# Where the tiles of an fp32r layer start in SBUF, and the form of its up-projection products

## The chip, the cores and the metric

The kernel runs on one core of one Trainium2 chip. The metric is the device time of one execution in microseconds (us). A profile belongs to one execution: its span goes from the first to the last instruction of the program, and the time of that execution contains a little more.

## The reference: what is computed

One decoder layer on x of 256 tokens by 2048 channels, all float32:

```
h   = rmsnorm(x, attn_norm_g)
z   = h @ w_in                   # pool channels | q | k | v | indexer q, k, weights
A   = pool_mixer(pool channels)  # causal means over 2, 4, 8, 16 tokens, then 256x256 products
B   = dsa_attention(q, k, v, ...)  # indexer scores, top 64 keys per query, softmax, 8 heads of 128
x1  = x + concat(A, B) @ w_out
up  = rmsnorm(x1, ffn_norm_g) @ w_up             # 2048 x 11264
c   = conv_b + causal depthwise conv of up, width 3
out = x1 + (silu(c[:, :5632]) * c[:, 5632:]) @ w_down   # 5632 x 2048
```

The weights are 203 MB, each is read once.

## The kernel before, in words

**Products in three parts.** To come near float32 accuracy, each operand is split into a high part (rounded to the fp32r type) and a low part (the rest), and a product is the sum of three: high by high, high by low and low by high, accumulated in PSUM. The split activations are the tiles `xhl` (16 row blocks of 128 channels, two parts, 256 tokens; 2048 bytes per block and partition), `yhl` (the mixer's and attention's output, same shape) and `ghl` (44 row blocks for w_down). `xhl` holds x first; after the out-projection the parts of x1 are written to the same tile (`x1_tr`, L608, by `split_x`, L119). The weights come in units of up to 1 MB through the sync engine's DMA queue into two `raw` buffers; a `Piece` (L93) is half a unit: ScalarE (ACT) rounds it into `whi` (L105), VectorE (DVE) subtracts into `wlo` (L106), with four buffers each, two pieces ahead of TensorE.

**Two roles.** In the token-major products (`mm_tok`, L210, products L222 to L224) the activations are the stationary operand, 128 tokens at a time, and a weight row of up to 512 columns moves: q, k, v and the indexer's columns (on `xhl`), the out-projection (on `yhl`) and the down-projection (on `ghl`). In the feature-major ones the weights are stationary, 128 columns at a time, and the 256 tokens move: the pool channels (`mm_feat1`, L231, three products of 256 columns, L233 to L235) and w_up (`mm_feat`, L226: one product of 512 columns with the two activation parts side by side, L228, and one of 256, L229). The products of the pool mixer (`pool_mix`, L579) use `mm_feat1` too. Each product brings its own load of the 128x128 stationary operand. The plain fp32 products and transposes of attention (L471, L483, L511, L523) run as two passes each.

**Order.** A loop at the end of `hybrid_kernel` walks over 385 pieces: per step it loads the unit three pieces ahead, splits the piece two ahead, runs the side work hung on this step by `at(step, ...)`, and then issues the piece's products. The order is w_in (indexer, k, pool, q, v interleaved), w_out, w_up for 44 blocks of 128 gate and 128 value columns, w_down in four groups of 512 columns. Attention, top-k and pooling are side work. In w_up the only side work on TensorE is `rows` of the second norm (L171, four passes of 128 columns, at its fifth step). A "block" below is one 128-row block of the contraction in w_up or in the pool channels: one stationary high part, one low part.

**After w_up's products.** Because high by high and high by low lie in separate halves of a 512-column PSUM row, `up_out` (L631) adds the halves: an ACT copy (L635), a DVE add (L636) and a DVE multiply by the norm's factor (L637) into `up`. `up_conv` and `up_gate` then make `ghl`.

**Places.** A tile's start in SBUF follows from what was allocated before it. Modulo 512 bytes, `xhl` starts at 256, `yhl` at 192, `ghl`, `whi` and `wlo` at 64 in this kernel. The blocks are multiples of 512 bytes, so all blocks of such a tile, both parts and both halves of the tokens start at the same place; a moving weight row of 512 columns does too.

Of the kernel before, what the change touches and what calls it, by code (L numbers as in the profile page):

```python
# [8 lines left out]
F32 = mybir.dt.float32  # L9
F32R = mybir.dt.float32r  # L10
BF16 = mybir.dt.bfloat16
AF = mybir.ActivationFunctionType
ALU = mybir.AluOpType
AX = mybir.AxisListType

P = 128
S = 256
D = 2048
KT = D // P
IH = 16  # L20
DFF = 5632
NF = DFF // P
# [7 lines left out]
C_AG, C_FG, C_PS, C_QG, C_KG, C_IC, C_CW, C_CB = 0, 16, 32, 40, 41, 42, 58, 58 + 3 * 2 * NF  # L30
# [9 lines left out]
WARM = 8  # L40


@with_exitstack
def hybrid_kernel(ctx, tc, xT, xN, par, wIa, wIb, wIc, wI2, wA, wU, wP, wO, wUp, wDn, out):
    nc = tc.nc
    PS = bass.MemoryType.PSUM

    cp = ctx.enter_context(tc.tile_pool(name="cp", bufs=1))
# [4 lines left out]
    pr = cp.tile([P, C_N], F32, name="pr")  # L53

    xf = cp.tile([P, KT, S], F32, name="xf")
    xt = xf.rearrange("p k t -> p (k t)").rearrange("p (a d) -> p a d", a=2)
    xhl = cp.tile([P, KT, 2, S], F32R, name="xhl")
    ga = cp.tile([P, KT], F32, name="ga")


# [32 lines left out]
    class Piece:  # L93


        def __init__(self, unit, a, b, mm):
            self.unit, self.a, self.b, self.mm = unit, a, b, mm
# [18 lines left out]
        sides.setdefault(step, []).append(lambda: f(*a))  # L116


    def split_x(k, src, gains, on_act):  # L119
        g = gains[:, k:k + 1]  # L120
        if on_act:
            nc.scalar.activation(xhl[:, k, 0], src, AF.Copy, scale=g)  # L122
        else:
            nc.vector.tensor_scalar(xhl[:, k, 0], src, g, None, op0=ALU.mult)
        nc.vector.scalar_tensor_tensor(xhl[:, k, 1], src, g, xhl[:, k, 0].bitcast(F32),  # L125
                                       op0=ALU.mult, op1=ALU.subtract)

    zp = ctx.enter_context(ExitStack())
    zc = zp.enter_context(tc.tile_pool(name="zc", bufs=1))
# [48 lines left out]
    r1, r2 = TokenNorm("r1"), TokenNorm("r2")  # L178
# [46 lines left out]

    def mm_feat(o, wh, wl, rhs, first, last):  # L226

        nc.tensor.matmul(o, wh, rhs.rearrange("p a t -> p (a t)"), start=first, stop=False)  # L228
        nc.tensor.matmul(o[:, 0:S], wl, rhs[:, 0], start=False, stop=last)  # L229

    def mm_feat1(o, wh, wl, rhs, first, last):  # L231

        nc.tensor.matmul(o[:, 0:S], wh, rhs[:, 0], start=first, stop=False)  # L233
        nc.tensor.matmul(o[:, 0:S], wh, rhs[:, 1], start=False, stop=False)  # L234
        nc.tensor.matmul(o[:, 0:S], wl, rhs[:, 0], start=False, stop=last)  # L235

    def tok_chunk(srcs, width, cuts=()):

        acc = Acc()
        for q in range(4):  # L240
            u = Unit(srcs[q], 4 * width, cuts[q] if q < len(cuts) else None)
            for h in range(2):
                def mm(p, k0=4 * q + 2 * h):
                    mm_tok(acc, p, (k0, k0 + 1), width)
                pieces.append(Piece(u, 2 * h * width, (2 * h + 2) * width, mm))
        return acc


    def pool_chunk(n):
        acc = Acc()  # L250
        for j in range(2):
            u = Unit(wU[2 * n + j], D)
            for h in range(2):
                def mm(p, j=j, h=h):
                    pt = acc.get()
                    for i in range(8):
                        k = 8 * h + i
                        mm_feat1(pt[:, j], *p.get(i * P, P), xhl[:, k], k == 0, k == KT - 1)
                pieces.append(Piece(u, h * 1024, (h + 1) * 1024, mm))
        return acc  # L260

    ia, za, ua, first = [], {}, [], {}
# [17 lines left out]
    for name in ORDER:  # L280
# [9 lines left out]
        else:  # L290
            c = ("k0", "k1", "q0", "q1", "v0", "v1").index(name)
            za[name] = tok_chunk([wA[c, q] for q in range(4)], 512)


    yhl = zc.tile([P, KT, 2, S], F32R, name="yhl")
    oa = []
    O0 = len(pieces)
    for c in range(4):
        acc = Acc()
        oa.append(acc)  # L300
        for q in range(4):
            u = Unit(wO[c, q], 2048)
            for h in range(2):
                def mm(p, acc=acc, k=4 * q + 2 * h):
                    mm_tok(acc, p, (k, k + 1), 512, yhl)
# [4 lines left out]
    for f in range(NF):  # L310
        us = [Unit(wUp[2 * f + j], D) for j in range(2)]
        seq = [(j, h) for j in range(2) for h in range(2)]
        if f == 0:
            seq = [(0, 0), (1, 0), (0, 1), (1, 1)]
        for j, h in seq:
            def mm(p, f=f, j=j, h=h):
                pt = ga_[f].get()
                for i in range(8):
                    k = 8 * h + i
                    mm_feat(pt[:, j], *p.get(i * P, P), xhl[:, k], k == 0, k == KT - 1)  # L320
            pieces.append(Piece(us[j], h * 1024, (h + 1) * 1024, mm))

    da = [Acc() for c in range(4)]
# [1 line left out]
    ghl = None  # L325
    for c in range(4):
        for m in range(NF // 2):
# [5 lines left out]
            o = (m % 2) * 1024  # L333
# [195 lines left out]
    pw_ = {}  # L529
# [49 lines left out]
    def pool_mix(n):  # L579
        g = GROUPS[n]  # L580
        hi, lo = pwt[n]
        for j in range(2):
            pt = ps_s.tile([P, 512], F32, name="pm", tag="ss")
            for k in range(2):
                c = slice(k * S + j * P, k * S + j * P + P)
                mm_feat1(pt, hi[:, c], lo[:, c], pw_[n][:, k], k == 0, k == 1)
            sc = pr[:, C_PS + 2 * g + j:C_PS + 2 * g + j + 1]
            y = yhl[:, 4 + 2 * n + 4 * (n == 3) + j]
            nc.scalar.activation(y[:, 0], pt[:, 0:S], AF.Copy, scale=sc)
            nc.vector.scalar_tensor_tensor(y[:, 1], pt[:, 0:S], sc, y[:, 0].bitcast(F32),  # L590
                                           op0=ALU.mult, op1=ALU.subtract)
# [16 lines left out]
    def x1_tr(c):  # L608
        for k in range(4 * c, 4 * c + 4, 2):
            tp = ps_s.tile([P, 512], F32, name="tp", tag="ss")  # L610
            for i in range(2):
                for th in range(2):
                    nc.tensor.transpose(tp[:, (2 * i + th) * P:(2 * i + th + 1) * P],  # L613
                                        xt[:, th, (k + i) * P:(k + i + 1) * P], ident)
            for i in range(2):
                split_x(k + i, tp[:, i * S:(i + 1) * S], pr[:, C_FG:C_FG + KT], True)


    fw = {}

    def ffn_open():
        nonlocal ghl
        zp.close()
        fp = ctx.enter_context(tc.tile_pool(name="fp", bufs=1))
        ghl = fp.tile([P, NF, 2, S], F32R, name="ghl")
        fw["up"] = [fp.tile([P, 2, S + 2], F32, name=f"up{i}") for i in range(2)]
        for u in fw["up"]:
            nc.gpsimd.memset(u[:, :, 0:2], 0.0)
        fw["fp"] = fp

    def up_out(f):  # L631
        fp = fw["fp"]
        pt = ga_[f].get()
        t = fp.tile([P, 2, S], F32, name="ft", tag="ft", bufs=2)
        nc.scalar.activation(t, pt[:, :, S:2 * S], AF.Copy)  # L635
        nc.vector.tensor_tensor(t, pt[:, :, 0:S], t, op=ALU.add)  # L636
        nc.vector.tensor_tensor(fw["up"][f % 2][:, :, 2:], t, r2.b2(), op=ALU.mult)  # L637

    def up_conv(f):
        u = fw["up"][f % 2]  # L640
# [62 lines left out]
    for n in range(4):  # L703
        st = first[f"u{n}"] + 4
        at(st, pool_u, n)
        at(st - 6, pool_w, n)
        at(st - 2, pool_ws, n)
        at(st + (n < 3), pool_win, n)
        at(st + 2 + 4 * (n < 3), pool_mix, n)
    for c in range(4):  # L710
        at(18 + 4 * c, load_xt, c)
        at(O0 + 8 * c + 8, x1_out, c)
        at(O0 + 8 * c + 9, x1_tr, c)
    at(G0 + 1, r2.cols_sq, ssq1)
    at(G0 + 2, r2.diag)
    at(G0 + 4, r2.rows)
    at(G0 + 2, ffn_open)
    for f in range(NF):
        st = G0 + 4 * f + 4
        at(st, up_out, f)  # L720
        at(st + 1, up_conv, f)
        at(st + 2, up_gate, f)
# [16 lines left out]
    def prep(n):  # L739
        if n < 15 and n % 2 == 1:  # L740
            for k in (n + 1, n + 2):
                split_x(k, xf[:, k], ga, True)
        if n < len(pieces):
            pieces[n].split(2 if n == 0 else 1)
        if n == 0:
            for k in range(2):
                split_x(k, xf[:, k], ga, False)
# [75 lines left out]
```

## Time and profile before

| | us |
|---|---|
| time, median of 3 runs | 1104.12 (1103.59 to 1105.32) |
| the profiled execution | 1104.05 |
| its span | 1102.2 |
| TensorE busy | 1094.5 (99%) |
| VectorE busy | 721.9 (65%) |
| ScalarE busy | 567.0 (51%) |
| mean granted TensorE clock | 0.999 |
| read from HBM | 203.25 MB, 186 GB/s |

A busy time counts the union of instructions that overlap. Matmuls are pipelined: the next begins before the shown end of the last, so their rate is read from the differences of their start times. The stages follow each other on TensorE: w_in to 265 us, w_out to 359 us, w_up to 858 us, w_down to 1098 us.

### The profile page before, as it was taken

To read this page: it belongs to the slowest core of one execution; us is meant where nothing else is said; L and a number is where in the kernel's file an instruction comes from. 1 tells how busy PE (TensorE), PEld (TensorE's weight loads), DVE (VectorE), ACT (ScalarE), POOL (GpSimd) and SP (SyncE) were. 2 spreads that over 40 slices of the span, in tenths; PEclk is the share of its full clock that TensorE was granted. 3 is DMA by queue.
4 is the path that set the end of the run, shared out by engine and by line. 5 is a ranking of instruction groups with operands and counts; after the bars stand their busy time and mean duration, and the time that the engine had idled before them with its cause. 6 is when DMAs were issued, how large, how long until landed. Compare 5 with 4: busy or idle time off the path is not lost.

```text
span 1102.2 us, 14803 instructions
## 1 busy us (share of the span) xinstructions
PE 1094.5 (99%) x5824; PEld 940.8 (85%) x5824; DVE 721.9 (65%) x1022; ACT 567.0 (51%) x797; POOL 12.9 (1%) x25
## 2 busy tenths in 40 slices
PE   8999999999999999999999999999999999999998
PEld 7988889889888888888888888888888888888886
DVE  7667867665555677777777777777777645444443
ACT  7555456654444655555555555555555433333331
POOL 0001000000000000000000000000000000000000
PEclk9999999999999999999999999999999999999999
DMA  8654564444554555555555555555555556565652
GB/s 284 245 190 141 180 235 153 163 163 157 186 174 171 191 192 190 181 180 181 189 187 191 191 189 182 181 180 190 187 191 191 191 191 210 191 210 191 215 191 91
DMA packets 32693, 206.30 MB, mean 187 GB/s; under 512 B 3696, under 2 KB 4080, under 8 KB 9584
## 3 DMA queue, kind: packets, MB, share of 16 engines
q1 hardware_dynamic: 31328, 203.25, 54.3%
q10 hardware_dynamic: 1296, 2.11, 0.5%
q8 instruction: 46, 0.75, 0.3%
q14 instruction: 23, 0.19, 0.1%
HBM read 203.25 MB, written 2.10 MB: 186 GB/s over the span
## 4 chain that ended last, share of the span: by engine, by line
PE 98%; DMA 1%; DVE 0%; ACT 0%; SPq 0%; issue 0%; DVEq 0%; ACTq 0%
PE mm L228 30%; PE mm L229 15%; PE mm L224 15%; PE mm L223 15%; PE mm L222 15%; PE mm L233 1%; PE mm L234 1%; PE mm L235 1%; PE sp L397 1%; DMA raw<-in_wI_dram 1%; DMA raw<-in_wIa_dram 1%; PE sp L483 0%; PE tp L613 0%; PE tp L471 0%; PE op L523 0%; PE tp L387 0%
## 5 line engine op out<-in xcount | busy, mean ns | idle before, releaser
L106 DVE TENSOR_TENSOR wlo<-raw,whi 128x1024 fp32r<-128x1024 f32 (+4 forms) x385 | 462.7, 1203 | 316.5 <-ACT whi L105 314.4
L105 ACT ACTIVATE whi<-raw 128x1024 fp32r<-128x1024 f32 (+4 forms) x385 | 400.1, 1041 | 440.9 <-PE mm L224 218.1
L228 PE MATMUL mm<-xhl,whi 128*128 128x512 f32 x1408 | 497.8, 397 | 0.0
L229 PE MATMUL mm<-xhl,wlo 128*128 128x256 f32 x1408 | 395.7, 281 | 0.0
L228 PEld LDWEIGHTS mm<-xhl,whi 128*128 128x128 f32 x1408 | 264.7, 188 | 65.3
L229 PEld LDWEIGHTS mm<-xhl,wlo 128*128 128x128 f32 x1408 | 264.3, 188 | 0.1
L222 PE MATMUL mm<-whi,ghl 128*128 128x512 f32 x352 | 136.9, 389 | 0.0
L224 PE MATMUL mm<-whi,ghl 128*128 128x512 f32 x352 | 136.9, 389 | 0.0
L223 PE MATMUL mm<-wlo,ghl 128*128 128x512 f32 x352 | 136.9, 389 | 0.0
L222 PE MATMUL mm<-whi,xhl 128*128 128x512 f32 (+3 forms) x288 | 108.6, 377 | 1.4 <-ACT xhl L122 0.8
L224 PE MATMUL mm<-whi,xhl 128*128 128x512 f32 (+3 forms) x288 | 107.3, 373 | 0.0
L223 PE MATMUL mm<-wlo,xhl 128*128 128x512 f32 (+3 forms) x288 | 106.8, 371 | 0.3 <-DVE wlo L106 0.3
L224 PEld LDWEIGHTS mm<-whi,ghl 128*128 128x128 f32 x352 | 66.1, 188 | 13.9
L222 PEld LDWEIGHTS mm<-whi,ghl 128*128 128x128 f32 x352 | 66.1, 188 | 13.8
L223 PEld LDWEIGHTS mm<-wlo,ghl 128*128 128x128 f32 x352 | 66.1, 188 | 13.5
L222 PEld LDWEIGHTS mm<-whi,xhl 128*128 128x128 f32 x288 | 54.1, 188 | 9.5 <-issue 1.2
L224 PEld LDWEIGHTS mm<-whi,xhl 128*128 128x128 f32 x288 | 54.1, 188 | 8.4 <-DVE xhl L125 0.5
L223 PEld LDWEIGHTS mm<-wlo,xhl 128*128 128x128 f32 x288 | 54.1, 188 | 8.0 <-DVE wlo L106 0.9
L222 PE MATMUL mm<-whi,yhl 128*128 128x512 f32 x128 | 50.9, 398 | 0.0
L224 PE MATMUL mm<-whi,yhl 128*128 128x512 f32 x128 | 50.5, 395 | 0.0
L223 PE MATMUL mm<-wlo,yhl 128*128 128x512 f32 x128 | 50.5, 394 | 0.0
L654 ACT ACTIVATE ghl<-fc 128x256 fp32r<-128x256 f32 x44 | 18.4, 418 | 57.0 <-DVE fc L653 57.0
(148 smaller groups left out, 843.9 us busy)
## 6 DMA issues: line engine op xcount, KB each, us to landing
raw<-in_wUp_dram SPq DMA_DIRECT2D x88, 1024.0 KB, 4.9
raw<-in_wDn_dram SPq DMA_DIRECT2D x44, 1024.0 KB, 4.9
raw<-in_wA_dram SPq DMA_DIRECT2D x24, 1024.0 KB, 4.9
raw<-in_wO_dram SPq DMA_DIRECT2D x16, 1024.0 KB, 4.9
raw<-in_wU_dram SPq DMA_DIRECT2D x8, 1024.0 KB, 4.9
raw<-in_wI_dram SPq DMA_DIRECT2D x4, 640.0 KB, 4.6
raw<-in_wIb_dram SPq DMA_DIRECT2D x3, 784.0 KB, 4.9
xf<-in_xT_dram SPq DMA_DIRECT2D x8, 256.0 KB, 5.2
```

What stands on the lines that cost most here:

```text
L105: i1 = nc.scalar.activation(hi, raw, AF.Copy)
L106: i2 = nc.vector.tensor_tensor(self.lo[:, c:c + n], raw, hi.bitcast(F32), op=ALU.subtract)
L222: nc.tensor.matmul(o, a[:, k, 0, t], wh, start=(k == 0), stop=False)
L223: nc.tensor.matmul(o, a[:, k, 0, t], wl, start=False, stop=False)
L224: nc.tensor.matmul(o, a[:, k, 1, t], wh, start=False, stop=(k == n - 1))
L228: nc.tensor.matmul(o, wh, rhs.rearrange("p a t -> p (a t)"), start=first, stop=False)
L229: nc.tensor.matmul(o[:, 0:S], wl, rhs[:, 0], start=False, stop=last)
L233: nc.tensor.matmul(o[:, 0:S], wh, rhs[:, 0], start=first, stop=False)
L234: nc.tensor.matmul(o[:, 0:S], wh, rhs[:, 1], start=False, stop=False)
L235: nc.tensor.matmul(o[:, 0:S], wl, rhs[:, 0], start=False, stop=last)
L397: nc.tensor.matmul(sp[:, a:b], q, kiT[:, e, 0:b - a], start=(e == 0), stop=(e == 1))
L654: nc.scalar.activation(ghl[:, f, 0], c[:, 0], AF.Copy)
```

## The change

A function `placed` allocates a tile with some more columns and gives a view that starts `o` float32 columns into it. With the offsets of `PLACE` x moves by 128 bytes to 384 modulo 512, `yhl` by 192 bytes to 384, and `ghl` by 320 bytes to 384. x1's parts get a view of their own in the same allocation as x, at offset 0, so they stay at 256. The weights' halves stay at 64. `mm_feat` is removed and `mm_feat1` takes its name, so a w_up block is three products of 256 columns, all added in the same 256 columns of PSUM. `up_out` has nothing left to add: one DVE multiply reads PSUM directly.

```diff
+PLACE = {"x": 32, "x2": 0, "y": 48, "g": 80}
+
+def placed(pool, n, name, o, of=None):
+    m = n * 2 * S
+    t = of[0] if of else pool.tile([P, m + (128 if name == "xhl" else o)], F32R, name=name)
+    return t, t[:, o:o + m].rearrange("p (k a t) -> p k a t", k=n, a=2)
...
-    xhl = cp.tile([P, KT, 2, S], F32R, name="xhl")
+    xhl = placed(cp, KT, "xhl", PLACE["x"])
+    x2hl = placed(cp, KT, "xhl", PLACE["x2"], xhl)
+    xhl, x2hl = xhl[1], x2hl[1]
...
-        nc.tensor.matmul(o, wh, rhs.rearrange("p a t -> p (a t)"), start=first, stop=False)
-        nc.tensor.matmul(o[:, 0:S], wl, rhs[:, 0], start=False, stop=last)
-
-    def mm_feat1(o, wh, wl, rhs, first, last):
-
         nc.tensor.matmul(o[:, 0:S], wh, rhs[:, 0], start=first, stop=False)
         nc.tensor.matmul(o[:, 0:S], wh, rhs[:, 1], start=False, stop=False)
         nc.tensor.matmul(o[:, 0:S], wl, rhs[:, 0], start=False, stop=last)
...
-    yhl = zc.tile([P, KT, 2, S], F32R, name="yhl")
+    yhl = placed(zc, KT, "yhl", PLACE["y"])[1]
...
-                    mm_feat(pt[:, j], *p.get(i * P, P), xhl[:, k], k == 0, k == KT - 1)
+                    mm_feat(pt[:, j], *p.get(i * P, P), x2hl[:, k], k == 0, k == KT - 1)
...
-                split_x(k + i, tp[:, i * S:(i + 1) * S], pr[:, C_FG:C_FG + KT], True)
+                split_x(k + i, tp[:, i * S:(i + 1) * S], pr[:, C_FG:C_FG + KT], True, x2hl)
...
-        ghl = fp.tile([P, NF, 2, S], F32R, name="ghl")
+        ghl = placed(fp, NF, "ghl", PLACE["g"])[1]
...
     def up_out(f):
-        fp = fw["fp"]
         pt = ga_[f].get()
-        t = fp.tile([P, 2, S], F32, name="ft", tag="ft", bufs=2)
-        nc.scalar.activation(t, pt[:, :, S:2 * S], AF.Copy)
-        nc.vector.tensor_tensor(t, pt[:, :, 0:S], t, op=ALU.add)
-        nc.vector.tensor_tensor(fw["up"][f % 2][:, :, 2:], t, r2.b2(), op=ALU.mult)
+        nc.vector.tensor_tensor(fw["up"][f % 2][:, :, 2:], pt[:, :, 0:S], r2.b2(), op=ALU.mult)
```

## Rows read from the trace of the kernel before

**Rows 1.** The page's busy times (part 1) and its chain of waits by line (part 4).
```profile
PE 1094.5 (99%) x5824; PEld 940.8 (85%) x5824; DVE 721.9 (65%) x1022; ACT 567.0 (51%) x797; POOL 12.9 (1%) x25
...
PE 98%; DMA 1%; DVE 0%; ACT 0%; SPq 0%; issue 0%; DVEq 0%; ACTq 0%
PE mm L228 30%; PE mm L229 15%; PE mm L224 15%; PE mm L223 15%; PE mm L222 15%; PE mm L233 1%; PE mm L234 1%; PE mm L235 1%; PE sp L397 1%; DMA raw<-in_wI_dram 1%; DMA raw<-in_wIa_dram 1%; PE sp L483 0%; PE tp L613 0%; PE tp L471 0%; PE op L523 0%; PE tp L387 0%
```

**Rows 2.** Stretch of w_up: us; busy PE, PEld, DVE, ACT, POOL; PEclk; DMA share; GB/s.
```profile
359.50:858.50 499.00, 499.00 (x2830) 433.59 (x2829) 375.76 (x530) 280.94 (x402) 0.84 (x3) 1.00 0.55 187
```

**Rows 3.** Instructions by line: ns (min/median/max), first and last start, forms.
```profile
L228 PE MATMUL mm<-xhl,whi x1408: 388/397/483, 359.5 to 858.0; 128*128 128x512 f32 x176
...
L222 PE MATMUL mm<-whi,ghl x352: 389/389/398, 858.3 to 1097.0; 128*128 128x512 f32 x176
```

**Rows 4.** Timeline of TensorE in w_up: start us, us, instruction.
```profile
599.68 0.40 PE L228 MATMUL mm<-xhl,whi 128*128 128x512 f32 x1
...
605.68 0.40 PE L228 MATMUL mm<-xhl,whi 128*128 128x512 f32 x1
```

**Rows 5.** Timeline of TensorE, pool products in a quick stretch.
```profile
115.93 0.28 PE L233 MATMUL mm<-xhl,whi 128*128 128x256 f32 x1
...
118.99 0.28 PE L233 MATMUL mm<-xhl,whi 128*128 128x256 f32 x1
```

**Rows 6.** Timeline of TensorE, pool products in a lagging stretch, and before it.
```profile
171.37 0.82 PE L483 MATMUL sp<-qk 128*128 128x128 f32 x4
...
172.38 0.28 PE L233 MATMUL mm<-xhl,whi 128*128 128x256 f32 x1
...
177.33 0.28 PE L233 MATMUL mm<-xhl,whi 128*128 128x256 f32 x1
```

**Rows 7.** Timeline of TensorE, pool products behind token-major products.
```profile
252.45 0.40 PE L224 MATMUL mm<-whi,xhl 128*128 128x512 f32 x1
252.69 0.28 PE L233 MATMUL mm<-xhl,whi 128*128 128x256 f32 x1
...
253.39 0.28 PE L233 MATMUL mm<-xhl,whi 128*128 128x256 f32 x1
...
253.73 0.28 PE L233 MATMUL mm<-xhl,whi 128*128 128x256 f32 x1
```

**Rows 8.** Timeline of TensorE, token-major products on xhl.
```profile
107.69 0.39 PE L222 MATMUL mm<-whi,xhl 128*128 128x512 f32 x1
...
110.44 0.39 PE L222 MATMUL mm<-whi,xhl 128*128 128x512 f32 x1
```

**Rows 9.** Timeline of TensorE, token-major products on yhl.
```profile
325.87 0.40 PE L222 MATMUL mm<-whi,yhl 128*128 128x512 f32 x1
...
329.35 0.40 PE L222 MATMUL mm<-whi,yhl 128*128 128x512 f32 x1
```

**Rows 10.** Timeline of TensorE, token-major products on ghl.
```profile
999.79 0.39 PE L222 MATMUL mm<-whi,ghl 128*128 128x512 f32 x1
...
1002.51 0.39 PE L222 MATMUL mm<-whi,ghl 128*128 128x512 f32 x1
```

**Rows 11.** Timeline of TensorE, plain fp32 products, two passes each.
```profile
264.92 0.59 PE L523 MATMUL op<-pT,zv 128*128 128x256 f32 x2
265.35 0.38 PE L524 MATMUL op<-pT,zv 128*128 128x128 f32 x2
```

**Rows 12.** Timeline of TensorE, the pool mixer's products.
```profile
140.92 0.28 PE L233 MATMUL pm<-dhl,pwh 128*128 128x256 f32 x1
...
142.00 0.39 PE L222 MATMUL mm<-whi,xhl 128*128 128x512 f32 x1
```

**Rows 13.** Longest wait in 380:850 (total, times, longest); the evacuation's two instructions.
```profile
ACT whi L105 <- PE mm L228: 149.8, 123, 1.6
...
L635 ACT ACTIVATE ft<-mm x44: 579/579/592, 373.1 to 859.4; 128x512 f32<-128x512 f32 x44
...
L636 DVE TENSOR_TENSOR ft<-mm,ft x44: 683/684/685, 374.1 to 860.7; 128x512 f32<-128x512 f32 x44
```

More of the change, by code (lines that the diff above doesn't have):

```diff
@@ L116, in at, with split_x @@
         sides.setdefault(step, []).append(lambda: f(*a))
-    def split_x(k, src, gains, on_act):
+    def split_x(k, src, gains, on_act, xhl=xhl):
         g = gains[:, k:k + 1]
@@ L257, in mm @@
                         k = 8 * h + i
-                        mm_feat1(pt[:, j], *p.get(i * P, P), xhl[:, k], k == 0, k == KT - 1)
+                        mm_feat(pt[:, j], *p.get(i * P, P), xhl[:, k], k == 0, k == KT - 1)
                 pieces.append(Piece(u, h * 1024, (h + 1) * 1024, mm))
@@ L585, in pool_mix @@
                 c = slice(k * S + j * P, k * S + j * P + P)
-                mm_feat1(pt, hi[:, c], lo[:, c], pw_[n][:, k], k == 0, k == 1)
+                mm_feat(pt, hi[:, c], lo[:, c], pw_[n][:, k], k == 0, k == 1)
             sc = pr[:, C_PS + 2 * g + j:C_PS + 2 * g + j + 1]
```

## The prediction

> **What bounds the kernel now.** I read the page's busy shares and its chain of waits first [rows 1]: TensorE is busy for 1094.5 of 1102.2 us, and 98% of the chain that ended last is TensorE work, with the w_up products (L228 and L229) at 45% and the three token-major products (L222 to L224) at another 45%. Nothing else is late over any length, so the time is the number of products times the spacing of their starts. The row by stage comes next [rows 2]: through w_up the granted clock is 1.00 of full speed, the 2.4 GHz level, and the DMA engines are busy 55% of the time. Nothing is lost to the clock. Then the first and last start of a kind of product [rows 3] and the timeline of TensorE, where the reader has to subtract start times (a matmul's shown length, 0.28 or 0.40 us, overlaps its successor and is no spacing):
>
> - w_up: 599.68 to 605.68 us holds 17 blocks of one 512- and one 256-column product, 353 ns each [rows 4]. From the first to the last start, 498.5 us over 1407 blocks is 354.3 ns, so this spacing holds for the whole stage.
> - the pool products, which already have the form of three 256-column products: 115.93 to 118.99 us is nine blocks, 340 ns each [rows 5].
> - the same line, same tiles, a little later: 172.38 to 177.33 us is 14 blocks, 353.6 ns each [rows 6].
> - token-major 512-column products: on xhl 107.69 to 110.44 us is twelve, 229 ns each [rows 8]; on yhl 3.48 us for fifteen, 232 ns [rows 9]; on ghl 2.72 us for twelve, 226.7 ns [rows 10], which the first and last start confirm: 238.7 us over 351 triples [rows 3].
>
> At 2.4 GHz, 512 columns are 213.3 ns and 768 columns 320 ns. So every kind of product pays 6 to 10% over its columns, and how much differs with the tile. Per 256 columns: 113.3 (pool, quick stretches; ghl), 114.6 (xhl), 116.0 (yhl), 117.8 ns (w_up; pool, lagging stretches). Two facts of the kernel stand beside that: a weight load is issued with every product, so TensorE reads two places at once, one moving and one stationary; and the start of these reads modulo 512 bytes is fixed for each tile. By the change's words and offsets the places before are 256 for x and x1, 192 for yhl, 64 for ghl, 64 for the weights' halves. The distance (moving minus stationary, modulo 512) is 0 for ghl, 384 for yhl, 320 for xhl as stationary, and 192 for w_up and the pool products, where the weights are stationary.
>
> **The change part by part.**
>
> *Form of the w_up block.* x1 stays at 256 and the weights at 64, so a w_up block becomes exactly a pool block of before, which ran at 340 ns in twelve of its sixteen stretches of eight blocks and at 353.6 in the other four. The two rates are steady once entered. Lagging stretches began twice, both times behind the four small products of L483 [rows 6]; the pool stretches that began behind a 512-column token-major product came out quick, one after two slower blocks: 0.70 us for two, then 340 ns [rows 7]. w_up is entered from a 512-column product as well, and is broken once, after twelve blocks or so, by the four small products of L171; in 1408 blocks it has nobody else between. I take the quick rate. 1408 x (353.3 - 340) = 18.7 us off. The bounds: 0 at the lagging rate; +7 us if a block took three times the 120 ns of the pool mixer's products, 1.08 us for nine, the slowest 256-column ones there are [rows 12]; -18.7 us is the most that a product of this kind shows; at 3 x 107.5 = 322.5 ns a block, what 256 cycles of the fp32 passes take [rows 11] (0.43 us for two passes of 512 cycles each), it would be -43 us.
>
> [...]
>
> *Evacuation of w_up.* The two halves no longer need adding: 44 ACT copies of 579 ns and 44 DVE adds of 684 ns go [rows 13], and the DVE multiply reads PSUM itself, which I price like the removed add (one PSUM and one SBUF operand, 684 ns). That is 25.5 us of ACT and 30.1 us of DVE saved off the path: ACT's splits of the weights wait for TensorE 123 times in the middle of the stage, 149.8 us in all [rows 13], so both engines run ahead. Value 0. What a faster TensorE asks of them: two 1 MB loads and four splits per 10.9 us instead of 11.3, a DMA share of 57% instead of 55% [rows 2]. No new wait.
>
> *Token-major products on moved tiles.* With x, yhl and ghl at 384, all 512-column products have distance 64 - 384 = 192. No token-major row of before has it. The nearest rows are those with distance 192 in the other role, weights stationary: 113.3 ns per 256 columns in the quick stretches, 117.8 in the lagging ones and in w_up; that is 226.7 or 235.6 ns per 512. I take 226.7, the value of the three-product form and of the one token-major tile that is steady. Against now: ghl 1056 x 0 = 0; yhl 384 x (232 - 226.7) = 2.0 us off; xhl 576 full-width x (229.2 - 226.7) = 1.4 us off; the 288 narrower ones wait on the first loads in part and count as 0. Sum -3.4 us. The ends: +14.1 us at 235.6 (1056 x 8.9 + 384 x 3.6 + 576 x 6.4 = 9.4 + 1.4 + 3.7 = 14.5, less rounding), and -26.6 us if all 2016 fell to 215 ns [rows 11] (another 11.7 ns each, 23.6 us).
>
> *Pool products.* x at 384 gives them distance 320. The row with 320 is xhl in the other role, 114.6 ns per 256 columns, 344 ns a block, against a mean of (96 x 340 + 32 x 353.6)/128 = 343.4 now: +0.1 us. Ends: -0.4 us (all quick) and +2.1 us (at 120 ns).
>
> *The tiles themselves.* Padding and a second view of xhl move no instruction and no DMA; 0, in both directions at most the noise.
>
> Sum: -18.7 - 3.4 + 0.1 = -22.0 us. The profiled execution took 1104.05 us, 1.85 us above its span and 0.07 below the median of 1104.12, so the forecast is 1104.05 - 22.0 = 1082 us.
>
> **The rivals.**
>
> 1. *Distance 192 is the lagging one* (other side). All 1408 blocks of w_up stand at 192 and run at the lagging rate, as do four pool stretches. If that rate belongs to 192, w_up gains nothing and the products moved to 192 come to 235.6 ns: +14.5 us, 1118.6 us. It decides from the point where w_up stays at 353 and a ghl product loses more than 2 ns (1056 x 2 = 2.1 us). Against it: twelve pool stretches at the same distance at 340.
> 2. *w_up locks at the lagging rate, the rest as forecast.* The small products of L171 set it off as L483 did, and nothing breaks it again; -3.3 us, 1100.8 us. For it: two lagging entries behind small products. Against: pool stretches behind L471 and those behind 512-column products were quick.
> 3. *The moved tiles do better than any row at full rate.* If at 192 the two reads of a token-major product stay out of each other's way, up to 23.6 us more goes; halfway is 1070, the end 1058 us. For it: 512 columns pay 13 ns or more over their 213.3, and the fp32 passes, which read at half the rate, pay 2. Against: no row has less than 226.
> 4. *Placement is nothing, and a product more costs its start.* The spacing of an fp32 pass over its columns is the only fixed price in the rows, about 2 ns (215 against 213.3): 1408 x 2 = 2.8 us more, 1107 us. [...] The spread of 226.7 to 232 ns for the same instruction on three tiles speaks against it.
>
> **Chances.** Forecast 0.58 (own range 1074 to 1091), rival 1 0.07, rival 2 0.12, rival 3 0.19, rival 4 0.04. A change under 0.2% (2.2 us) can't be told from none here. Faster: forecast, rival 3 and most of rival 2, 0.85. Same: 0.05, mostly rival 2 with a loss elsewhere. Slower: rivals 1 and 4, less rounding, 0.10. The range: 1060 leaves out the far end of rival 3, and 1102 holds rival 2 and leaves out rivals 1 and 4.
>
> **What would show it.** The timeline of TensorE in w_up: 340 ns from one block's first product to the next one's, 479 us for the stage; 353 is rival 2. In the down stage the starts of L222 to L224: 226.7 ns is the forecast, 235 rival 1, under 222 rival 3. yhl's row must lose its 232. ACT and DVE must lose 25 and 30 us without TensorE gaining an idle gap; a gap in front of w_up products that waits for a weight half or for the evacuation would mean that an off-path engine became the bound. If w_up's spacing is neither 340 nor 353, the account by two rates is wrong.

## The result and the profile after

The changed kernel took 1113.91 us (median of 4, 1113.17 to 1114.51) against 1103.88 beside it: ratio 1.0088, 95% interval 1.007 to 1.0105. The forecast was 1082 us, with a range of 1060 to 1102. Ratios here and below leave out slow executions, of which there were two, 1815 and 2205 us, among the ten of `best_r3`, one of the experiments. The profiled execution took 1113.17 us, its span is 1111.5.

TensorE is still the bound: busy 99%, and 10.7 us longer than in [rows 1]. The page's busy times:

```profile
PE 1105.2 (99%) x7232; PEld 1007.4 (91%) x7232; DVE 695.2 (63%) x978; ACT 546.1 (49%) x753; POOL 12.8 (1%) x25
```

The first and last start of the token-major products on ghl (L237 is the former L222):

```profile
L237 PE MATMUL mm<-whi,ghl x352: 392/396/398, 860.5 to 1106.2; 128*128 128x512 f32 x176
```

The down-projection takes 245.7 us from first to last start, 700 ns per triple or 233.3 ns per product, against 238.7 us in [rows 3]: 7.0 us of the loss. It also starts 2.2 us later, at 860.5 instead of 858.3.

The timeline of TensorE, one row per product, start and length in us (L243 to L245 are the three 256-column products, L186 those of the norm's rows):

```profile
115.93 0.28 PE L243 MATMUL mm<-xhl,whi 128*128 128x256 f32 x1
...
119.11 0.28 PE L243 MATMUL mm<-xhl,whi 128*128 128x256 f32 x1
...
107.85 0.40 PE L237 MATMUL mm<-whi,xhl 128*128 128x512 f32 x1
...
110.65 0.40 PE L237 MATMUL mm<-whi,xhl 128*128 128x512 f32 x1
...
326.25 0.39 PE L237 MATMUL mm<-whi,yhl 128*128 128x512 f32 x1
...
329.05 0.39 PE L237 MATMUL mm<-whi,yhl 128*128 128x512 f32 x1
...
362.12 0.28 PE L243 MATMUL mm<-xhl,whi 128*128 128x256 f32 x1
...
371.87 0.28 PE L243 MATMUL mm<-xhl,whi 128*128 128x256 f32 x1
...
373.57 0.28 PE L243 MATMUL mm<-xhl,whi 128*128 128x256 f32 x1
...
373.91 0.60 PE L186 MATMUL pb<-dg,ones 128*128 128x128 f32 x4
...
375.06 0.28 PE L243 MATMUL mm<-xhl,whi 128*128 128x256 f32 x1
...
375.41 0.28 PE L243 MATMUL mm<-xhl,whi 128*128 128x256 f32 x1
...
599.78 0.28 PE L243 MATMUL mm<-xhl,whi 128*128 128x256 f32 x1
...
605.43 0.28 PE L243 MATMUL mm<-xhl,whi 128*128 128x256 f32 x1
...
999.84 0.40 PE L237 MATMUL mm<-whi,ghl 128*128 128x512 f32 x1
...
1002.64 0.40 PE L237 MATMUL mm<-whi,ghl 128*128 128x512 f32 x1
```

To be seen, by subtraction: nine pool blocks in 3.18 us, 353 ns each, where [rows 5] has 340. Twelve products on xhl in 2.80 us, 233.3 ns, against 229 in [rows 8]; twelve on yhl in 2.80, 233.3 against 232 in [rows 9]; twelve on ghl in 2.80 against 2.72 in [rows 10]. And w_up: it starts at the forecast rate, five blocks from 371.87 to 373.57 us, 340 ns each. Then come the four passes of L186, and behind them a block takes 350 to 360 ns; at 599.78 to 605.43 us sixteen blocks take 5.65 us, 353 ns, the rate of [rows 4] in another form. Up to 860.5 us it stays there. The stage, 362.1 to 860.5 us, is 498.4 us long, 0.4 less than before. So of 9.3 us of span 7.0 are lost in w_down, 2.6 ahead of w_up (its first product starts at 362.12 us instead of 359.5 in [rows 3]), and 0.4 came back in w_up; 0.1 is rounding.

The row of w_up by stage (us, busy PE, PEld, DVE, ACT, POOL, granted clock, DMA share, GB/s), and the waits in 380 to 850 us (total, times, longest), to compare with [rows 2] and [rows 13]:

```profile
362.10:860.50 498.40, 498.40 (x4237) 498.37 (x4236) 349.83 (x487) 260.11 (x358) 0.84 (x3) 1.00 0.53 187
```

```profile
ACT whi L120 <- PE mm L244: 160.1, 117, 1.8
...
DVE up L643 <- PE mm L245: 23.0, 41, 0.6
...
ACT whi L120 <- DMA raw<-in_wUp_dram: 5.8, 3, 2.1
```

DVE and ACT lost 26 and 21 us of busy time in the stage, the clock is at 1.00, and ACT still waits for TensorE 117 times. Two waits are new, DVE's for the end of a block's products and, three times, ACT's for a load of weights. Neither held TensorE up: it is busy for 498.40 of the stage's 498.40 us. So the cause lies in the spacing of the products themselves.

### The profile page after: what moved, and what is told of

Same layout as the page of the kernel before. It is cut to its first block, busy times and chain, and to the rows that moved or that the text cites. A ratio compares the mean times of both kernels' runs of the same rounds, so it can differ in the third digit from the quotient of the medians.

```text
span 1111.5 us, 17447 instructions
## 1 busy us (share of the span) xinstructions
PE 1105.2 (99%) x7232; PEld 1007.4 (91%) x7232; DVE 695.2 (63%) x978; ACT 546.1 (49%) x753; POOL 12.8 (1%) x25
## 4 chain that ended last, share of the span: by engine, by line
PE 99%; DMA 0%; SPq 0%; DVE 0%; ACT 0%; issue 0%; DVEq 0%; ACTq 0%
PE mm L245 16%; PE mm L244 16%; PE mm L243 16%; PE mm L237 16%; PE mm L239 16%; PE mm L238 15%; PE sp L407 1%; DMA xf<-in_xT_dram 0%; PE sp L493 0%; PE tp L481 0%; PE tp L623 0%; PE op L533 0%; PE tp L521 0%; PE tp L397 0%; PE pm L244 0%; PE pm L243 0%
## 5 line engine op out<-in xcount | busy, mean ns | idle before, releaser
L243 PE MATMUL mm<-xhl,whi 128*128 128x256 f32 x1536 | 432.5, 282 | 0.0
L245 PE MATMUL mm<-xhl,wlo 128*128 128x256 f32 x1536 | 431.3, 281 | 0.0
L244 PE MATMUL mm<-xhl,whi 128*128 128x256 f32 x1536 | 431.3, 281 | 0.0
L244 PEld LDWEIGHTS mm<-xhl,whi 128*128 128x128 f32 x1536 | 294.3, 192 | 0.2
L243 PEld LDWEIGHTS mm<-xhl,whi 128*128 128x128 f32 x1536 | 288.3, 188 | 0.2
L245 PEld LDWEIGHTS mm<-xhl,wlo 128*128 128x128 f32 x1536 | 288.3, 188 | 0.0
L239 PE MATMUL mm<-whi,ghl 128*128 128x512 f32 x352 | 139.2, 396 | 0.0
L237 PE MATMUL mm<-whi,ghl 128*128 128x512 f32 x352 | 139.2, 395 | 0.0
L238 PE MATMUL mm<-wlo,ghl 128*128 128x512 f32 x352 | 139.2, 395 | 0.0
L237 PE MATMUL mm<-whi,xhl 128*128 128x512 f32 (+3 forms) x288 | 109.7, 381 | 0.5 <-ACT xhl L137 0.4
L237 PEld LDWEIGHTS mm<-whi,ghl 128*128 128x128 f32 x352 | 66.2, 188 | 15.9
L237 PEld LDWEIGHTS mm<-whi,xhl 128*128 128x128 f32 x288 | 54.3, 189 | 9.4 <-ACT whi L120 1.0
L237 PE MATMUL mm<-whi,yhl 128*128 128x512 f32 x128 | 50.9, 398 | 0.0
```

The lines of the kernel that those rows point to most:

```text
L237: nc.tensor.matmul(o, a[:, k, 0, t], wh, start=(k == 0), stop=False)
L238: nc.tensor.matmul(o, a[:, k, 0, t], wl, start=False, stop=False)
L239: nc.tensor.matmul(o, a[:, k, 1, t], wh, start=False, stop=(k == n - 1))
```

## The experiments

Three theories to begin with. **A**: a product's spacing follows from the distance of its moving and its stationary tile; at the distance of w_up a stream of three-product blocks has two steady rates, 113.3 and 117.8 ns per product, and a break of the stream by other products picks one. **B**: the moved or lengthened tiles slow w_up in another way, or (**C**) a third product just costs its start. The places below are modulo 512 bytes, the weights' halves at 64 where nothing else is said. L243 and its neighbours keep their numbers in these kernels.

**The form alone** (`form_only`).

```diff
-PLACE = {"x": 32, "x2": 0, "y": 48, "g": 80}
+PLACE = {"x": 0, "x2": 0, "y": 0, "g": 0}
```

> Only the form of the w_up block changes: x, x1 at 256, yhl at 192, ghl at 64 as before. Theory A (the rate of a three-product block is held from where it is entered, and the small products of the norm's rows throw it to 353 ns): w_up 340 ns for about 32 blocks, then 353; ghl products 226.7 ns, xhl 229, yhl 232; time that of before, 1103 to 1105 us. Theory B (the moved places slow w_up through something else than its own tiles): w_up at 340 throughout, 1086 us. Theory C (a third product costs its start): about 1107 us.

Measured: 1103.31 us, ratio 0.9998 (0.9988 to 1.0007). The form by itself is worth nothing here, and costs nothing either, which is against C. w_up's last block starts at 858.0 us, as in [rows 3]:

```profile
L243 PE MATMUL mm<-xhl,whi x1536: 276/281/471, 113.3 to 858.0; 128*128 128x256 f32 x192
```

One point of A's expectation failed: w_up was at 118 ns already from its transposes (L623) to the norm's rows, not at 113.3.

**The places alone** (`places_only`): the changed kernel with `mm_feat`'s products of 512 and 256 columns and the addition in `up_out` for w_up.

> Only the places change, as in the changed kernel; w_up keeps its products of 512 and 256 columns and the addition behind them. Theory A: w_up 353 ns as before; ghl 233.3, xhl 231, yhl 233.5 ns, so +7.0, +1.2 and +0.5 us and the pool at 353 (+1.2 us): 1113 to 1115 us, the whole loss. If the form has a part in the loss, the time is clearly under 1113.

Measured: 1114.18 us, ratio 1.0095 (1.008 to 1.011); xhl, yhl and ghl at 233.3 ns each. The whole loss is the places'.

**Two idle transposes behind the norm's rows**, in the form alone (`form_relock`) and in the changed kernel (`after_relock`).

```diff
     at(G0 + 4, r2.rows)
+    at(G0 + 4, relock)
...
+    def relock():
+        tp = ps_s.tile([P, 512], F32, name="tp", tag="ss")
+        for i in range(2):
+            nc.tensor.transpose(tp[:, i * P:(i + 1) * P], ident, ident)
```

> As form_only, and two idle transposes of the identity behind the products of the norm's rows, ahead of the next w_up block (0.4 us of extra TensorE work, no one reads them). Theory A: pool stretches behind transposes were all at 340 ns in the kernel before, so w_up goes on at 340 to its end: 1104 - 18 = 1086 us. Theory B and a rate that belongs to the length of the stage: 353 ns again and the time of form_only.

> The changed kernel with the same two transposes. Theory A: w_up 340 ns to its end, 1114 - 18 = 1096 us; the moved tiles' products stay at 231 to 234 ns. Rival: what slows w_up is its distance of 192, whatever entered it: 1114 us.

Measured: `form_relock` 1084.85 us, ratio 0.9831 (0.9816 to 0.9845). Work that no one reads made the kernel 18.5 us faster than `form_only`. The break in its timeline, and the first and last start of the blocks' first product:

```profile
372.02 0.38 PE L632 MATMUL tp<-ident 128*128 128x128 f32 x2
...
L243 PE MATMUL mm<-xhl,whi x1536: 276/276/471, 113.1 to 839.8; 128*128 128x256 f32 x192
```

Behind the break at 372.02 us stand 1376 blocks, and the last one starts at 839.8 us: 340 ns each. `after_relock` took 1114.07 us, ratio 1.0094 (1.0079 to 1.0109): there the same transposes left w_up at 353. So the quick rate is to be had at a distance of 192, and transposes are no switch that always sets it.

**Many breaks in one stage** (`form_kicks`, `after_kicks`): no transposes behind the rows, but ahead of every sixth gate/value block.

```diff
-    at(G0 + 4, relock)
+    for f in range(6, NF, 6):
+        at(G0 + 4 * f, relock)
```

> The kernel with the form alone, no transposes behind the norm's rows, but two idle transposes ahead of every sixth gate/value block of w_up (seven places, the first after 96 blocks of products). Theory A (two steady rates, and a break of the stream picks one): each of the eight stretches of w_up stands at 113.3 or 117.8 ns per product throughout, and changes only at a break; the first stretch is at 117.8 as in the kernel with the form alone. Rival (the rate drifts with buffers or traffic, and the relocked kernel was quick by what the transposes delayed): changes of rate inside stretches, or none at the breaks.

> The changed kernel with the same seven breaks. Theory A: as in the one above, stretches at 113.3 or 117.8 ns, the first at 117.8 behind the norm's rows, and at least one of the seven breaks brings 113.3, since the tiles of w_up have the same distance. Rival (the view of x1 beside x, or the longer xhl, keeps w_up slow): 117.8 in all.

Measured: 1088.54 and 1112.65 us, a single execution each and so without an interval. In both, every stretch between two breaks stands at one rate, 113.3 or 117.8 ns in its first and in its second half. In `form_kicks` all seven breaks gave 113.3; in `after_kicks` the first of them gave 113.3, the second took it away again, and the rest left 117.8. Those two breaks in the timeline of `after_kicks`:

```profile
431.19 0.38 PE L632 MATMUL tp<-ident 128*128 128x128 f32 x2
...
432.46 0.28 PE L243 MATMUL mm<-xhl,whi 128*128 128x256 f32 x1
...
432.80 0.28 PE L243 MATMUL mm<-xhl,whi 128*128 128x256 f32 x1
...
496.04 0.28 PE L243 MATMUL mm<-xhl,whi 128*128 128x256 f32 x1
...
496.38 0.28 PE L243 MATMUL mm<-xhl,whi 128*128 128x256 f32 x1
...
496.72 0.38 PE L632 MATMUL tp<-ident 128*128 128x128 f32 x2
...
497.30 0.28 PE L243 MATMUL mm<-xhl,whi 128*128 128x256 f32 x1
...
497.65 0.28 PE L243 MATMUL mm<-xhl,whi 128*128 128x256 f32 x1
```

Behind the first break, at 431.19 us, a block takes 340 ns (432.46 to 432.80); the second break turns 340 (496.04 to 496.38) into 350 (497.30 to 497.65). No rate changes inside a stretch, which is against the rival, a drift with buffers or traffic; and the 192 quick blocks of `after_kicks` are against the view of x1 keeping w_up slow.

**The scan of places** (`scan1`, `scan2`, `scan3`, `fine`), all with three products in w_up, `PLACE` changed alone. (An offset also moves what is allocated behind the tile in its pool: with yhl most tiles of attention and of the mixer, with ghl `up`.)

> Three-product w_up; x at 0, x1 at 64, yhl at 128, ghl at 320 modulo 512, weights at 64 (moving minus stationary: 64 for xhl, 448 for yhl, 256 for ghl; 0 for w_up). Theory P (the rate of a product follows from the distance of the two tiles): none of the three token-major stages keeps the value it had in the kernels so far (229.3 or 233.3, 232.4 or 233.3, 226.5 or 233.1 ns), each has its own between 213 and 236. Theory S (the stage decides, not the place): 229, 232, 226 to 233 again.

> Three-product w_up; x at 448, x1 at 128, yhl at 64, ghl at 32, weights at 64. Theory P: yhl, now at ghl's old distance of 0, takes ghl's 226.5 ns instead of 232; theory S: 232 again. ghl at a distance of 32, beside its old one, shows how wide the good place is: 226 if wider than 32 bytes.

> Three-product w_up; x at 96, x1 at 0, yhl at 288, ghl at 480, weights at 64: distances 480, 288 and 96 for the token-major products, 448 for w_up. Theory P: xhl at 480 lies beside distance 0 and comes near 226; yhl at 288 between 229 (320) and what 256 gives; the rest of the scan, no number.

> Three-product w_up; x at 80, yhl at 72, ghl at 68, x1 at 272 modulo 512, weights at 64: distances -16, -8 and -4 bytes for the token-major products and 208 for w_up. Theory P in its narrow form (distance 0 modulo 256 alone is good): ghl at -4 already at 233. If a line of 16 bytes or more counts, ghl and yhl keep 226.5 and x leaves it. No theory here gives under 226 ns; that would be a new place.

Measured ns per 512-column token-major product, worked out from starts in the timelines, by moving minus stationary modulo 512:

| distance | ns | tile |
|---|---|---|
| 0 | 226.7 | ghl at 64; yhl at 64 |
| 256 | 226.7 | ghl at 320; yhl at 320 |
| 64; 320 | 229.5; 229.4 | xhl at 0; at 256 |
| 128; 384 | 232.8; 232.4 | xhl at 448; yhl at 192 |
| 192; 448 | 233.3; 233.4 | xhl, yhl, ghl at 384; yhl at 128 |
| 32; 288 | 233.3; 233.3 | ghl at 32; yhl at 288 |
| 96 | 233.3 | ghl at 480 |
| 480 | 233.2 | xhl at 96 |
| -4; -8; -16 | 232.4; 230.7; 232.6 | ghl at 68; yhl at 72; xhl at 80 |

The five pairs 256 bytes apart agree within 0.4 ns, and nothing is under 226.7: the place that ghl had before was one of the two best, and 384 one of the worst. In `scan2` (yhl at 64, ghl at 32) twelve products on yhl take 2.72 us, and the 351 triples of ghl 245.7 us, as in the changed kernel:

```profile
326.35 0.39 PE L237 MATMUL mm<-whi,yhl 128*128 128x512 f32 x1
...
329.07 0.39 PE L237 MATMUL mm<-whi,yhl 128*128 128x512 f32 x1
...
L237 PE MATMUL mm<-whi,ghl x352: 393/395/403, 859.4 to 1105.1; 128*128 128x512 f32 x176
```

w_up at distance 0 (`scan1`, x1 at 64) has a rate of its own, 120.0 ns per product through all its breaks; here five blocks take 1.80 us, while ghl at 320 takes 238.7 us:

```profile
600.01 0.28 PE L243 MATMUL mm<-xhl,whi 128*128 128x256 f32 x1
...
601.81 0.28 PE L243 MATMUL mm<-xhl,whi 128*128 128x256 f32 x1
...
L237 PE MATMUL mm<-whi,ghl x352: 389/389/396, 867.1 to 1105.8; 128*128 128x512 f32 x176
```

At 64 (`scan2`) w_up stood at 117.8, at 448 (`scan3`) at 113.3 behind the rows, at 208 (`fine`) at 119.2. The times of these four, 1112.78, 1112.05, 1095.76 and 1117.51 us in a single execution each, follow from that. Of the expectations, ghl at -4 leaving 226.5 spoke for the narrow form, though 230.7 at -8 fits no form; the guess that xhl at 480 comes near 226 was wrong (233.2).

**Every tile 128 bytes further** (`shift128`): weights' halves at 192, x and x1 at 384, yhl at 320, ghl at 192.

```diff
-PLACE = {"x": 32, "x2": 0, "y": 48, "g": 80}
+PLACE = {"x": 32, "x2": 32, "y": 0, "g": 0}
...
-    tab = cp.tile([P, 1], F32, name="tab")
+    tab = cp.tile([P, 33], F32, name="tab")[:, 0:1]
```

> All tiles 128 bytes further, weights' halves at 192, x and x1 at 384, yhl at 320, ghl at 192: every distance is that of the kernel with the form alone, every place is another. Theory P (distance): xhl 229, yhl 232, ghl 226.5 ns and w_up 117.8 ns per product, as there. Theory A2 (the place itself modulo 512 decides): xhl at 384 takes 233 as in the changed kernel, yhl and ghl other values too.

Measured: 1103.83 us in a single execution, xhl 229.3, yhl 232.6, ghl 226.7 ns, w_up 117.8. Twelve products on xhl:

```profile
107.62 0.39 PE L237 MATMUL mm<-whi,xhl 128*128 128x512 f32 x1
...
110.37 0.39 PE L237 MATMUL mm<-whi,xhl 128*128 128x512 f32 x1
```

2.75 us: for the token-major products the distance decides, not the place; xhl stands at 384 here and pays 229.

**Both gains together.** yhl at 320 (the weights' distance 256), x and x1 at 256, ghl at 64; two transposes behind the rows (`best`), one (`best_r1`), three (`best_r3`), yhl at 64 (`best_y64`), breaks behind the rows and ahead of blocks 2, 4, 6 and 8 (`best_five`).

> x and x1 at 256, yhl at 320, ghl at 64, three products per w_up block, the two transposes behind the norm's rows. The scan gave 226.5 ns for a token-major product at a distance of 0 or 256, and 229.4 at 64 or 320. Theory P: yhl falls from 232.4 to 226.5 or 227 ns, 384 x 5.6 = 2.1 us; with w_up at 113.3 ns 1084.85 - 2.1 = 1082.7 us. If the break behind the rows does not give 113.3 with this allocation, 1101 us.

> x and x1 at 256, yhl at 320, ghl at 64, three-product w_up, one idle transpose behind the norm's rows instead of two. yhl 227 ns in any case. Theory A with the break's length as the chooser: another length, another rate: 113.3 ns and 1082.5 us. If the history ahead of the break chooses, 117.8 and 1101.5 us as with two.

> The same with three idle transposes. Length as the chooser: 113.3 or 117.8, not the same as with one and two transposes both; history: 117.8 and 1101.9 us.

> yhl at 64 instead of 320, two transposes. The distance to the weights is 0 instead of 256, both good for yhl (227 ns); what enters w_up then is the same stream. If the history is what chooses and it is the same, 1101.7 us as with yhl at 320; at 113.3 ns it would be 1082.5.

> yhl at 320, breaks of two transposes behind the norm's rows and ahead of blocks 2, 4, 6 and 8 of w_up: five draws. Theory A: the rate behind the last break holds to the end of w_up, 1083.5 to 1085.5 us if it is 113.3 (each break costs some 0.4 us), 1102 to 1103 us if it is 117.8.

Measured: ratios 0.9985 (0.9976 to 0.9994), 0.9988 (0.9979 to 0.9997), 0.999 (0.9979 to 1.0), 0.9986 (0.9977 to 0.9995) and 0.9995 (0.9986 to 1.0004). yhl fell to about 227 ns in each, 2 us, as expected; w_up stood at 117.8 behind every break. `best` at its break, and its first and last start:

```profile
369.49 0.38 PE L632 MATMUL tp<-ident 128*128 128x128 f32 x2
...
L243 PE MATMUL mm<-xhl,whi x1536: 276/281/476, 112.2 to 855.5; 128*128 128x256 f32 x192
```

From 369.49 to 855.5 us are 1376 blocks of 353 ns. `best` issues what `form_relock` issues; only yhl and the tiles allocated behind it, most of attention's and the mixer's, lie 128 bytes further. Yet six of the ten pool stretches, all ahead of the first product on yhl, run at the other rate. They do so in every kernel here with these places (`best_r1`, `best_r3`, `best_five`, `draws` and `last`), and none of the four traces with the old places does (before, `form_only`, `form_relock`, `form_kicks`). The stretch behind the transposes of zq and zk, first in `form_only`, then in `best`:

```profile
178.59 0.28 PE L243 MATMUL mm<-xhl,whi 128*128 128x256 f32 x1
...
180.63 0.28 PE L243 MATMUL mm<-xhl,whi 128*128 128x256 f32 x1
```

```profile
177.50 0.28 PE L243 MATMUL mm<-xhl,whi 128*128 128x256 f32 x1
...
179.62 0.28 PE L243 MATMUL mm<-xhl,whi 128*128 128x256 f32 x1
```

Six blocks take 2.04 us, 340 ns each, and 2.12 us, 353 ns each: places of tiles that the blocks themselves do not read bear on the rate that a break leaves.

**Breaks of many lengths** (`draws`): `best` with no transposes, and fourteen idle bf16 products, each ahead of a gate/value block.

```diff
+    def relock(n):
+        tp = ps_s.tile([P, 512], F32, name="tp", tag="ss")
+        nc.tensor.matmul(tp[:, 0:n], warm[:, 0:P], warm[:, 0:n], start=True, stop=True)
...
+    for f, n in [(2, 256), (5, 258), (8, 260), (11, 262), (14, 264), (17, 266), (20, 268), (23, 270), (26, 272), (29, 128), (32, 136), (35, 384), (38, 392), (41, 64)]:
+        at(G0 + 4 * f, relock, n)
```

> x and x1 at 256, yhl at 320, ghl at 64, three-product w_up, no transposes behind the norm's rows; instead fourteen breaks in w_up, each one idle bf16 product, of 256, 258, 260, 262, 264, 266, 268, 270, 272, 128, 136, 384, 392 and 64 columns in turn. If a break picks the rate by the delay that it puts between two blocks, some of the widths bring 113.3 ns and others leave or bring 117.8; if the history ahead of w_up holds through every break, all fifteen stretches are at 117.8.

Measured: 1096.29 us in a single execution. Behind the norm's rows, with nothing added, 113.3 ns; then 117.8 behind 256, 258, 262, 266, 268, 270, 128 and 136 columns, and 113.3 behind 260, 264, 272, 384, 392 and 64. Seven of fifteen stretches are quick, with no order in the lengths that I can read. The history ahead of w_up does not outlast every break.

**No idle work at all** (`last`).

```diff
-PLACE = {"x": 32, "x2": 0, "y": 48, "g": 80}
+PLACE = {"x": 0, "x2": 0, "y": 32, "g": 0}
```

> The changed kernel with other places alone: x and x1 at 256, yhl at 320, ghl at 64; no idle products anywhere. Up to the norm's rows it issues what the kernel with the fourteen breaks issues, where the stretch behind the rows ran at 113.3 ns: if a break's outcome is reproducible, w_up holds 113.3 ns to its end and the time is 1103.5 - 18.5 - 2.1 = 1083 us. If the outcome is not tied to the instructions issued, w_up is at 117.8 and the time 1101.5 us, or it differs between executions by 18 us.

Measured: 1083.40 us (five executions, 1083.34 to 1083.54), ratio 0.9815 (0.9801 to 0.9828). It beats both kernels, by 20 and 30 us, and differs from the changed one by three numbers. Its timeline, and the first and last start of L243:

```profile
329.85 0.39 PE L237 MATMUL mm<-whi,yhl 128*128 128x512 f32 x1
...
333.25 0.39 PE L237 MATMUL mm<-whi,yhl 128*128 128x512 f32 x1
...
369.46 0.60 PE L186 MATMUL pb<-dg,ones 128*128 128x128 f32 x4
...
L243 PE MATMUL mm<-xhl,whi x1536: 275/276/476, 112.6 to 837.4; 128*128 128x256 f32 x192
```

Fifteen products on yhl in 3.40 us, 226.7 ns each. The four passes of L186 follow here too, but the 1376 blocks behind them, from 369.46 to 837.4 us, take 340 ns each. Against `best`, the two idle transposes are all that differs: they add 0.2 us of work and 18 us of time.

## Why the prediction was wrong

- *The bound, and spacing as the measure*: right. Nearly every change of time in these kernels is a change of spacing on TensorE.
- *Form of the w_up block*, -18.7 us: the step failed at "I take the quick rate". Its size was right: `form_relock` and `last` have the 340 ns and the 18.5 us. But the changed kernel holds 340 for 32 blocks and 353 for 1376, and the stage gave back 0.4 us. The text said that w_up "is broken once" by L171's products and took the pool stretches behind 512-column products as the measure. What counts is the last break, since the rate behind it holds for the rest of the stage; the entry counts for 8 blocks. With 1376 blocks behind one break, twelve of sixteen stretches was no ground for 0.58. Rival 2 had this, mechanism and place, at 0.12; its reason does not hold in general, since the same small products left 353 here and 340 in `last`.
- *Token-major products on moved tiles*, -3.4 us: failed, it was +9.7 us (ghl 1056 x 6.6 = 7.0, xhl 576 x 4.0 = 2.3, yhl 384 x 0.9 = 0.4). The quick rate of the reversed roles was carried over to a distance that no token-major row had. The reversed roles don't give the same value: at 192 a token-major product has one rate, 233.3 ns, neither 226.7 nor 235.6, and at 0 it is at its best where w_up is at its worst (120.0). Its ends were summed a little wrong: 14.5 us, as rival 1 has it, not 14.1, and 23.6 + 3.4 = 27.0, not 26.6.
- *Pool products at distance 320*, +0.1 us: +1.3 (353.3 instead of a mean of 343.4 ns a block); inside the bounds. These terms ahead of w_up make 4.0 us, measured were 2.6; most of the rest was given back where the first loads set the pace (0.8 us in the 400-column products, counted as 0).
- *Evacuation*, 0: right. The DVE multiply from PSUM took 692 ns (684 assumed). DVE and ACT lost 26.7 and 20.9 us of busy time, less than the 30.1 and 25.5 forecast, off the path.
- *Rival 1*, 1118.6 us: the nearest in time, and right that the moved tiles lose; wrong that 192 itself sets w_up's rate, since `form_relock` and `last` run at 340 there.
- *Rival 3*: nothing under 226.7 ns was found at any distance. *Rival 4*: `form_only` at 0.9998 rules out 2 ns a block.

Two readings of the rows, behind the first of these steps, were wrong as well. In w_up the stream is broken twice: ahead of L171, after eight blocks, come the eight transposes of L613 (362.34 us below), which the description of the kernel leaves out too. And behind L483's products there are four entries of pool stretches, not two: two are lagging, and two are quick, one of them shown below. So the trace before already showed that the kind of product in a break does not fix the rate.

```profile
181.19 0.82 PE L483 MATMUL sp<-qk 128*128 128x128 f32 x4
...
182.54 0.28 PE L233 MATMUL mm<-xhl,whi 128*128 128x256 f32 x1
...
184.24 0.28 PE L233 MATMUL mm<-xhl,whi 128*128 128x256 f32 x1
...
362.34 1.03 PE L613 MATMUL tp<-ident,xf 128*128 128x128 f32 x8
```

From 182.54 to 184.24 us are five blocks of 340 ns. The upper bound of the step was summed wrong: at 120 ns per product it is 1408 x (360 - 353.3) = 9.4 us, not 7.

The Trainium skill's page "TensorE: Matmul & The Clock Gate", section "Back-to-back issue gap", gives columns over 2.4 plus 2.5 ns as the gap of an isolated product at full speed, and for products in a stream a measured 131 ns or so per 512 columns, with no data type beside it. The traces here have neither: 512 fp32r columns took 226.7 to 233.4 ns in a stream, and the same 256 columns 113.3, 117.8 or 120.0 ns, with the granted clock at 1.00. The Trainium skill's page "SBUF — State Buffer", section "Who interferes with whom", lists two read ports of TensorE, one for the moving operand and one for the weight load, as independent. The scan differs in so far as the distance of the two operands alone moves a token-major product by 6.7 ns.

What stays open: what in a break picks the rate. It is reproducible (`last` within 0.2 us over five executions, `best` within 1.3 over eleven), it is not the kind of product alone (transposes gave 340 and 353), and idle products of fourteen lengths, each tried once, show no order. Nor do the instructions and the distance of the blocks' own tiles fix it: `best` differs from `form_relock` in the places of yhl and of the tiles behind it alone, and in `shift128`, where the instructions and the distances of the weights to xhl, yhl and ghl are those of `form_only`, two pool stretches and the entry of w_up took the other rate. Which of the moved tiles does it, and how, was not tried. Nor was it tried whether the weight load or the moving read is the one that waits.

## What to carry to other kernels

Where TensorE is the bound, measure the spacing of its products per tile and compare it with columns over clock; where it differs between tiles, shift one operand by fractions of 256 bytes and measure again, in the same role, since neither the other role nor another width gives the value. If a stream shows two rates in one trace, look for the last break before its long stretch, and predict from that break, not from the share of stretches. A product inserted ahead, or a tile moved that the stream does not read, can then move the time by more than its own cost, so a small edit has to be timed in the whole kernel.

## What was not expected of the hardware

- The distance of the two operands in SBUF repeats with 256 bytes: five pairs of places within 0.4 ns, over a spread of 226.7 to 233.4 ns.
- Two steady rates of one instruction stream at the same places of its tiles (distance 192): 340.0 and 353.3 ns per block, held over up to 1376 blocks and exchanged only at breaks.
- Some steady values are multiples of 6.67 ns over their pattern: 340 = 51, 353.3 = 53, three ghl products 680 = 102 or 700 = 105, three on xhl 687 = 103 times. Others are not, as three products on yhl at 192 (697 = 104.6 times) or a w_up block at a distance of 208 (357.6 = 53.6 times), so this is a remark and no rule.
